# The projection behind the attention as seven products of quarters: its first two products beside the last head, the sample last

## The chip, the cores and the metric

The kernel runs on one core of one Trainium2 chip. The metric is the device time of one execution in microseconds (us). The profile is one execution taken by the hardware profiler; matrix products run on TensorE (PE), elementwise work on VectorE (DVE), ScalarE (ACT) and GpSimd (POOL), and most transfers are issued from SyncE (SP).

## The reference, cut to what matters

One encoder layer is applied to a prompt of 1024 tokens and to a sample of 256 tokens (D_MODEL = 1024, four attention heads of 256, all float32). The part that the change touches is the last line of the cross-attention, `o @ w_o`, and the residual sum behind it:

```python
def memory_cross_attention(h, mem, w_q, w_kv, w_o):
    ...
    o = jnp.einsum('bhlm,bmhd->blhd', p, v).reshape(bsz, seq, D_MODEL)
    return o @ w_o

    x = x + merged @ w_out
    x = x + memory_cross_attention(rmsnorm(x, norm_xa_w), rmsnorm(mem, norm_mem_w), xa_w_q, xa_w_kv, xa_w_o)
    h = rmsnorm(x, norm_ffn_w)
    gu = h @ ffn_w_gate_up
    x = x + (jax.nn.silu(gu[..., :D_FF]) * gu[..., D_FF:]) @ ffn_w_down
```

## The kernel before

Activations lie transposed: 128 features on the partitions, eight such tiles (`KT`), and the tokens along the free dimension in three blocks, `BLOCKS`: two of 512 (the prompt) and one of 256 (the sample). To keep float32 accuracy, each operand is split into a high part (a rounding copy on ScalarE) and a low part (a subtraction on VectorE or GpSimd, `split`), and `mm3` makes each product of three matmuls: high x high, high x low, low x high.

TensorE's order is the order of the program text, written by hand. A stage is a generator run by `K.main`; side generators (`K.side`) are advanced from it when a clock, which counts the matmuls issued so far, reaches their due time. So the attention of a head (`attend`) is threaded between the matmuls of the stage that runs as main. The other engines' instructions are ordered by the framework's planner by readiness, with the program order as priority, and each engine then runs its list in that order.

The stages around the change: `out_proj` (from line 1426) is the projection of the merged branches. For the prompt it already works by seven products of quarters (class `Seven`, line 1200, a Strassen-like scheme): the 1024x1024 weight is taken as four quarters of 512x512, the input as four quarters (two halves of the features by two token blocks), and seven products of sums of quarters (`p1` to `p7`) take the place of eight. The sums of weights (`wsum`) are on GpSimd, those of inputs (`xsum`) on VectorE; `wsplit` and `xsplit` make the high and low parts. Behind it come the four heads: each has two tiles of the query projection (`tile_of`), beside which the head before is attended. The output of heads 0 to 2 goes through the DRAM tensor `od`.

The projection behind the attention is the class `OutProj` (line 1347): eight tiles of output features by three token blocks, each a sum over eight tiles of input features. Its `begin` runs four of these (m, b) pairs over the first six input tiles beside the last head; the outputs of heads 0 to 2 are read back from `od` as `oraw` and split into `o_h`, and the last head's output is split into `o_h` directly. `run` finishes these four, does the rest, adds the residual from the DRAM tensor `x1d` on VectorE, sums the squares for the norm (`nms`), and stores `x2d`. The norm of each block (`rest`) makes the high and low parts `h3` for the FFN, which starts with `ff_first` (line 1954). `first_weights` and `after` load and split the FFN's first weights during the projection.

Of the kernel before, what the change touches and what calls it, by code (L numbers as in the profile page):

```python
# [17 lines left out]
P = 128  # L18
# [145 lines left out]
def trunk_kernel(ctx: ExitStack, tc: tile.TileContext, a):  # L164
# [40 lines left out]
    order += [(a["w_o"][m], "wp" if m < 2 else "wx") for m in range(KT)]  # L205
# [994 lines left out]
    class Seven:  # L1200


        def __init__(self, w, p, mt, smp):
            self.w, self.p, self.mt, self.smp = w, p, mt, smp
            self.raw = {}
            self.forms = [hp.tile([P, 2, 4, 512], F32R, tag=tag, name="xf") for tag in ("hi1", "lo1")]
            self.wf = {}

# [3 lines left out]
        def load(self, i, j, x, raw=None):  # L1212
            raw = self.room(f"r{i}{j}{x}") if raw is None else raw
# [3 lines left out]
        def wsplit(self, ph, src, x, eng, tags=None):  # L1217
            if x == 0:
                self.wf[ph] = []
            if ph in ("p1", "p6", "p7", "p3"):  # L1220
                hl = tuple(wp.tile([P, 1024], F32R, tag=tag, name=tag) for tag in ("whi", "wlo"))
            else:
                hl = tuple(self.room(tag, F32R) for tag in tags or (f"ah{x}", f"al{x}"))
            with ExitStack() as st:
                if ph == "p5":
                    st.enter_context(tc.issue_after(self.after))
                S.activation(hl[0], self.raw[*src, x], AF.Copy)
            eng.tensor_tensor(out=hl[1], in0=self.raw[*src, x], in1=f32(hl[0]), op=ALU.subtract)  # L1228
# [15 lines left out]
        def prep(self, ph, x):  # L1244
            w, sub = (0, 0), ALU.subtract
            if ph == "p1":
                self.wsplit(ph, (0, 0), x, V)
            elif ph == "x1":
                self.xsplit(0, 0, 0, x)
            elif ph == "x5":  # L1250
                self.xsum((0, 0), (0, 1), (0, 0), x)
                self.xsplit(1, 0, 0, x)
            elif ph == "p5":
                self.wsum((0, 1), (0, 1), (1, 1), x, ALU.add)
                self.wsplit(ph, (0, 1), x, G)
            elif ph == "c6":
                self.wsum((0, 1), (0, 1), (0, 0), x, sub)
                self.xsum((0, 0), (1, 1), (0, 0), x)
            elif ph == "p6":
                self.wsplit(ph, (0, 1), x, V)  # L1260
                self.xsplit(0, 0, 0, x)
            elif ph == "c7":
                self.wsum((0, 0), (1, 1), (0, 1), x, sub)
                self.xsum((0, 1), (1, 1), (0, 1), x)
# [357 lines left out]
    qes.close()  # L1622

# [715 lines left out]
```

## Time and profile before

| what | value |
|---|---|
| median of 3 runs | 2236.93 us (2235.42 to 2237.05) |
| the profiled execution | 2239.41 us, of which the span is 2237.6 us |
| TensorE busy in the span | 2186.0 us (98%), 12416 matmuls, mean granted clock 0.996 |
| VectorE, ScalarE, GpSimd busy | 1439.1, 829.3, 559.9 us |
| the projection behind the attention | its first matmul at 1257.04 us, the FFN's first at 1391.91 us |

Times inside the profile count from the span's start. A row of an engine's timeline gives the start, the duration, the engine and line, the operation with its output and inputs, the shapes and the count; what stands in brackets is the idle time before it and what ended that. In the busy table each row is a stretch of time with the busy time and the number of instructions of each engine, then TensorE's granted clock, and the share and rate of the DMA engines.

### The profile page before, as it was taken

To read this page: it belongs to the slowest core of one execution; us is meant where nothing else is said; L and a number is where in the kernel's file an instruction comes from. 1 tells how busy PE (TensorE), PEld (TensorE's weight loads), DVE (VectorE), ACT (ScalarE), POOL (GpSimd) and SP (SyncE) were. 2 spreads that over 40 slices of the span, in tenths; PEclk is the share of its full clock that TensorE was granted. 3 is DMA by queue.
4 is the path that set the end of the run, shared out by engine and by line. 5 is a ranking of instruction groups with operands and counts; after the bars stand their busy time and mean duration, and the time that the engine had idled before them with its cause. 6 is when DMAs were issued, how large, how long until landed. Compare 5 with 4: busy or idle time off the path is not lost.

```text
span 2237.6 us, 32329 instructions
## 1 busy us (share of the span) xinstructions
PE 2186.0 (98%) x12416; PEld 1909.1 (85%) x12416; DVE 1439.1 (64%) x2796; ACT 829.3 (37%) x1481; POOL 559.9 (25%) x358
## 2 busy tenths in 40 slices
PE   6999999999999999999999999999999999999998
PEld 5988888888888899788888888888888888888888
DVE  7767788897985874588844536743444344478575
ACT  5434143333423443124544433432223223243453
POOL 3010000000000000025331332466666666200031
PEclk9999999999999999999999999999999999999999
DMA  5222322214234454981431342222222222393531
GB/s 180 82 80 74 104 72 83 73 62 112 68 103 128 149 150 129 314 283 47 152 103 48 137 162 78 67 104 85 83 86 80 76 83 90 134 355 127 202 109 57
DMA packets 192821, 263.52 MB, mean 118 GB/s; under 512 B 72394, under 2 KB 102682, under 8 KB 192666
## 3 DMA queue, kind: packets, MB, share of 16 engines
q1 hardware_dynamic: 172826, 232.34, 31.7%
q10 hardware_dynamic: 19840, 29.11, 3.6%
q8 instruction: 97, 1.59, 0.3%
q14 instruction: 58, 0.48, 0.1%
HBM read 183.24 MB, written 78.16 MB: 117 GB/s over the span
## 4 chain that ended last, share of the span: by engine, by line
PE 77%; DVE 10%; issue 5%; DMA 4%; ACT 2%; POOL 1%; SPq 0%; ACTq 0%; POOLq 0%; DVEq 0%
PE bank L108 76%; DMA tbd<-stage 1%; PE bank L121 1%; DVE acc L615 1%; DVE xf L126 1%; DVE W L761 1%; DVE wlo L126 1%; DMA braw<-gq 1%; DVE x L1437 1%; DVE wlo L1228 1%; DMA t<-sgd 0%; DVE sw L919 0%; DVE W L764 0%; DVE U L861 0%; DVE lo L126 0%
## 5 line engine op out<-in xcount | busy, mean ns | idle before, releaser
L108 PE MATMUL bank<-hi,whi 128*128 128x512 f32 (+1 forms) x1976 | 701.8, 355 | 0.0
L108 PE MATMUL bank<-hi,wlo 128*128 128x512 f32 (+1 forms) x1976 | 687.0, 348 | 0.0
L108 PE MATMUL bank<-lo,whi 128*128 128x512 f32 (+1 forms) x1976 | 686.8, 348 | 0.0
L108 PEld LDWEIGHTS bank<-hi,wlo 128*128 128x128 f32 x1976 | 373.5, 189 | 48.8
L108 PEld LDWEIGHTS bank<-hi,whi 128*128 128x128 f32 x1976 | 374.4, 189 | 43.9 <-issue 0.2
L108 PEld LDWEIGHTS bank<-lo,whi 128*128 128x128 f32 x1976 | 374.5, 190 | 43.3 <-issue 0.2
L125 ACT ACTIVATE whi<-raw 128x1024 fp32r<-128x1024 f32 (+1 forms) x136 | 137.1, 1010 | 262.8 <-PE bank L108 221.4
L126 POOL TENSOR_TENSOR wlo<-raw,whi 128x1024 fp32r<-128x1024 f32 x65 | 157.5, 2426 | 302.8 <-ACT whi L125 302.8
L108 PE MATMUL bank<-bhl,whi 128*128 128x512 f32 x408 | 125.9, 390 | 0.0
L126 DVE TENSOR_TENSOR wlo<-raw,whi 128x1024 fp32r<-128x1024 f32 (+1 forms) x71 | 81.6, 1151 | 43.7 <-ACT whi L125 36.7
L126 POOL TENSOR_TENSOR wlo<-x,whi 128x1024 fp32r<-128x1024 f32 x40 | 97.5, 2436 | 46.8 <-ACT whi L125 46.7
L2009 DVE TENSOR_TENSOR x<-x,bank 128x512 f32<-128x512 f32 x21 | 14.4, 688 | 125.3 <-ACT x L1804 125.3
L108 PEld LDWEIGHTS bank<-bhl,whi 128*128 128x128 f32 x408 | 76.4, 188 | 16.3 <-ACT whi L125 0.3
L615 DVE SCALAR_TENSOR_TENSOR acc<-craw,sm,acc 128x510 f32<-128x510 f32 (+1 forms) x96 | 73.5, 766 | 20.5 <-ACT acc L613 19.1
L1817 DVE SCALAR_TENSOR_TENSOR t<-t,x 128x512 f32<-128x512 f32 x42 | 64.4, 1534 | 28.4 <-ACT t L1816 28.4
L108 PE MATMUL bank<-bhl,wlo 128*128 128x512 f32 x204 | 79.6, 390 | 0.5 <-DVE wlo L126 0.5
L761 DVE TENSOR_TENSOR W<-W,UT 128x2 f32<-128x2 f32 (+30 forms) x155 | 73.0, 471 | 11.0 <-DMA W<-in_eye 6.7
L250 DVE TENSOR_TENSOR nacc<-nacc,nsq 128x512 f32<-128x512 f32 (+1 forms) x68 | 57.9, 852 | 34.5 <-ACT nsq L249 33.4
L125 ACT ACTIVATE whi<-x 128x1024 fp32r<-128x1024 f32 (+1 forms) x48 | 49.0, 1025 | 79.9 <-PE bank L108 73.7
L1826 DVE SCALAR_TENSOR_TENSOR t<-bank,t 128x512 f32<-128x512 f32 (+1 forms) x44 | 24.5, 558 | 82.6 <-PE bank L108 82.6
L978 ACT ACTIVATE gs<-bank 128x512 f32<-128x512 f32 (+1 forms) x60 | 31.2, 520 | 124.9 <-PE bank L108 119.6
L881 POOL COPY UT<-U 64x512 f32<-64x512 f32 x20 | 13.9, 699 | 247.2 <-PE bank L108 245.6
(372 smaller groups left out, 4606.6 us busy)
## 6 DMA issues: line engine op xcount, KB each, us to landing
raw<-in_w_gu SPq DMA_DIRECT2D x44, 512.0 KB, 3.4
braw<-gq SPq DMA_DIRECT2D x14, 1024.0 KB, 6.5
raw<-in_w_g SPq DMA_DIRECT2D x20, 512.0 KB, 3.3
gq<-t SPq DMA_DIRECT2D x33, 256.0 KB, 2.0
gtd<-gs ACTq DMA_DIRECT2D x32, 256.0 KB, 2.0
w<-in_w_dn SPq DMA_DIRECT2D x8, 1024.0 KB, 12.3
raw<-in_w_qkv SPq DMA_DIRECT2D x12, 512.0 KB, 3.5
gq<-r SPq DMA_DIRECT2D x22, 256.0 KB, 2.1
```

The lines of the kernel that those rows point to most:

```text
L108: self.nc.tensor.matmul(out, l, r, start=start, stop=stop, skip_group_check=more)
L121: self.nc.tensor.transpose(out, x, ident)
L125: self.last_hi = self.nc.scalar.activation(hi, src, AF.Copy).ins
L126: (eng or self.nc.vector).tensor_tensor(out=lo, in0=src, in1=f32(hi), op=ALU.subtract)
L250: (eng or V).tensor_tensor(out=self.acc, in0=self.acc, in1=sq, op=ALU.add)
L615: V.scalar_tensor_tensor(out=dst, in0=src, scalar=wj, in1=dst, op0=ALU.mult, op1=ALU.add)
L761: V.tensor_tensor(out=t3, in0=u3[:, i:, c:].rearrange("p j c -> p c j"), in1=XL[:, 32 * i + i : 32 * i + 32].unsqueeze(1).to_broadcast([P, ...
L978: S.activation(t, ps, AF.Tanh, scale=0.5)
L1228: eng.tensor_tensor(out=hl[1], in0=self.raw[*src, x], in1=f32(hl[0]), op=ALU.subtract)
L1437: V.scalar_tensor_tensor(out=d, in0=ps, scalar=0.5, in1=d, op0=ALU.mult, op1=ALU.add)
L1817: V.scalar_tensor_tensor(out=t, in0=t, scalar=1.0, in1=src, op0=ALU.add, op1=ALU.mult)
L1826: V.scalar_tensor_tensor(out=out, in0=u, scalar=sign, in1=t, op0=ALU.mult, op1=ALU.mult)
```

## The change

`OutProj`, `FIRST_PS`, `first_weights` and `after` go. The prompt's part of `o @ w_o` is made by `Seven` too, through the functions `o_begin` and `o_proj`; `Seven` gets its rooms and engines as arguments (`raws`, `places`, `engs`), and the steps of its `prep` are named by kind (`w` split of a weight, `x` split of an input, `s` sum of weights, `d` difference of inputs) and product. The heads' outputs for the prompt are kept unsplit in `mo`: those of heads 0 to 2 are read from `od`, the last head's are copied there by ScalarE. `o_begin` runs the products p1 and p5 beside the last head and copies their sums to `s12` (ScalarE); `o_proj` runs p6, p2, p7, p4 and p3, adds the kept sums into the residual (four operations on VectorE, four on GpSimd), and then runs the four sample products from `od`. The heads' keys and values move to the pool `comb`, whose rooms later hold quarters of `w_o`, their forms and FFN operands. The FFN's first weights are loaded and split among the sample's products. The norms get waiting times of their own, `LAGO`.

```diff
-    order += [(a["w_o"][m], "wp" if m < 2 else "wx") for m in range(KT)]
...
-                for mt in range(2):
-                    vs = slice((2 * g + mt) * 256 + j * P, (2 * g + mt) * 256 + (j + 1) * P)
...
-                if o_h is None:
+                if mt is None or b == 2:
                     oo = tp.tile([P, 512], F32, tag="oo", name="oo", bufs=2)[:, :n]
                     S.activation(oo, po, AF.Copy)
                     S.dma_start(od[2 * h + j, :, t0 : t0 + n], oo)
                 else:
-                    hi, lo = o_h[b]
-                    split(hi[:, 2 * h + j, :], lo[:, 2 * h + j, :], po)
+                    S.activation(mt[b][:, 2 * h + j, :], po, AF.Copy)
                 yield A4
+            if b == 1 and then is not None:
+                then()
...
+            mo = [hp.tile([P, KT, 512], F32, tag=tag, name="mo") for tag in ("hi0", "lo0")]
+            wq = [tq.tile([P, 2, NTOK], F32R, tag=f"q{i}", name="wq") for i in range(2)]
+            tag = lambda *x: tuple(f"t{i}" for i in x)
+            form = (tag(4, 6), tag(5, 7))
+            oo_ = Seven(
+                a["w_o"], tpool, mo, None, {(0, 1): tag(0, 1), (1, 1): tag(2, 3), (1, 0): tag(8, 9)},
+                dict(p5=lambda x: tuple(t[:, x, :1024] for t in wq), p2=form, p4=form, s01=(tag(0, 2), tag(1, 3)),
+                     s10=lambda x: (slot(8 + x), slot(10 + x)), s00=form),
+                dict(p5=G, p2=G, p4=G, s01=G, s10=G))
+            for k in range(0, 6, 2):
+                for b in range(2):
+                    SY.dma_start(mo[b][:, k : k + 2, :], od[k : k + 2, :, 512 * b : 512 * b + 512].rearrange("k p t -> p k t"))
+                if k == 0:
+                    for x in range(2):
+                        oo_.load(0, 0, x, K.raw()[:, :1024])
+                elif k == 2:
+                    for x in range(2):
+                        oo_.load(0, 1, x)
+                        oo_.load(1, 1, x)
+            oo_.preps("wp1", "xp1")
+            def then():
+                oo_.preps("dp6", "xp6")
...
+    def kept(i, scale=1.0):
+        return lambda m, ps: S.activation(s12[i][:, m, :], ps, AF.Copy)
+    def o_begin():
+        oo_.preps("dp5", "xp5")
+        for y in range(2):
+            oo_.prep("sp5", y)
+            oo_.prep("wp5", y)
+        oo_.preps("sp6")
+        yield from oo_.prompt("p1", 0, pa, True, kept(0))
+        oo_.preps("wp6")
+        yield from oo_.prompt("p5", 1, pa, False, kept(1))
...
-    K.main(op.begin())
+    K.main(o_begin())
     K.finish(at_side)
...
+    def second_weights():
+        for n, (i, j) in enumerate(((8, 9), (10, 11))):
+            gu_w[1, 3 * n] = slot(i), slot(j)
+            split(*gu_w[1, 3 * n], gu_raw[1][n], G)
+        g, u = gu_raw[1]
+        for x, y in ((u[:, 512:], u[:, :512]), (u[:, :512], g[:, :512]), (g[:, :512], u[:, 512:]), (g[:, 512:], g[:, :512])):
+            G.tensor_tensor(out=x, in0=x, in1=y, op=ALU.add)
+    def o_proj():
+        x = [p.tile([P, KT, n], F32, tag=f"x{b}", name=f"x{b}") for b, (p, (_, n)) in enumerate(zip((x0p, xhp, x2p), BLOCKS))]
+        for b in (1, 0, 2):
+            t0, n = BLOCKS[b]
+            SY.dma_start(x[b], x1d[:, :, t0 : t0 + n])
...
+        for y in range(2):
+            oo_.load(1, 0, y)
+        pa = [bank(pm) for _ in range(4)]
+        both("wp2", "xp2")
+        both("sp7", "dp7")
+        add(1, 0, 1, V)
+        add(0, 0, 0, V)
+        yield from oo_.prompt("p6", 0, pa, True, into(0, 1, False))
+        both("wp7", "xp7")
+        both("dp4", "sp3")
+        add(1, 1, 1, G)
+        add(0, 1, 0, G)
+        smp = [hp.tile([P, KT, NS], F32R, tag=tag, name="smp") for tag in ("lo2", "hi2")]
...
+        pb = [bank() for _ in range(4)]
+        yield from oo_.prompt("p2", 1, pb, True, into(0, 0, True))
+        both("wp4", "xp4")
+        for y in range(2):
+            oo_.load(0, 1, y, K.raw()[:, :1024])
+        yield from oo_.prompt("p7", 0, pa, False, into(1, 1, True))
+        both("wp3", "xp3")
+        oo_.preps("ws01")
+        for k in (4, 0):
+            sl = slice(k, k + 4)
+            split(smp[0][:, sl, :], smp[1][:, sl, :], f32(smp[1][:, sl, :]), G)
+        yield from oo_.prompt("p4", 1, pa, False, into(1, 0, True))
...
+        norm_of(0)
+        oo_.preps("ws10")
+        pb = [bank(pm) for _ in range(4)]
+        yield from oo_.prompt("p3", 0, pb, True, into(0, 1, True))
+        norm_of(1)
+        yield from oo_.sample("p4", 1, into_s(1, False))
+        oo_.preps("ws00")
+        gu_load(0, wp)
+        yield from oo_.sample("s01", 0, into_s(1, True))
+        for i in (0, 3):
+            gu_w[0, i] = pair_of(wp)
+            split(*gu_w[0, i], gu_raw[0][i // 3], G)
+        gu_load(1, wp)
+        comb_rooms(b12, ((0, 1), (2, 3)))
+        yield from oo_.sample("s10", 1, into_s(0, False))
+        second_weights()
+        yield from oo_.sample("s00", 0, into_s(0, True))
...
-    K.main(op.run(x1d, 1.0, S_FFN, x2p, x2d, sinks, first_weights, after))
-    room, x1 = op.x[0], op.x[1]
+    K.main(o_proj())
+    room, x1 = ox[0], ox[1]
...
+LAGO = (5000, 7000, 6000)
```

298 lines of the change are left out of this document (129 added, 169 removed).

## The prediction

> **What bounds the kernel now.** I read the page first, then the busy table by stage, then the rows of each engine around the stage that the change rebuilds.
>
> ```profile
> PE 2186.0 (98%) x12416; PEld 1909.1 (85%) x12416; DVE 1439.1 (64%) x2796; ACT 829.3 (37%) x1481; POOL 559.9 (25%) x358
> ...
> PEclk9999999999999999999999999999999999999999
> ...
> PE 77%; DVE 10%; issue 5%; DMA 4%; ACT 2%; POOL 1%; SPq 0%; ACTq 0%; POOLq 0%; DVEq 0%
> ```
>
> TensorE is the bound: it is busy nearly all of the span, at full clock, and 77% of the chain that ended last is its own. So a matmul taken out is worth its slot, as long as nothing else becomes late. Whether something does is a question for the stage. The busy table, in order: the earlier stage that already multiplies by seven products; 26 us inside it; the last head until the projection is alone; the rest of the projection; the first part of the FFN.
>
> ```profile
> core 0: us, PE busy (x) PEld busy (x) DVE busy (x) ACT busy (x) POOL busy (x), PEclk, DMA share, GB/s
> 993.40:1094.80 101.40, 100.70 (x531) 85.91 (x530) 81.08 (x86) 48.79 (x64) 49.14 (x19) 1.00 0.32 112
> 1003.20:1029.20 26.00, 26.00 (x138) 22.34 (x137) 24.91 (x16) 9.40 (x9) 24.68 (x8) 1.00 0.26 95
> 1257.04:1291.80 34.76, 31.92 (x187) 27.09 (x186) 23.90 (x53) 14.99 (x37) 9.96 (x5) 1.00 0.33 110
> 1291.80:1392.10 100.30, 100.22 (x542) 87.05 (x542) 51.24 (x85) 29.86 (x46) 36.04 (x18) 1.00 0.30 106
> 1392.10:1436.00 43.90, 42.56 (x225) 36.44 (x225) 42.80 (x66) 22.13 (x36) 13.92 (x8) 1.00 0.23 77
> ```
>
> Today's projection (fourth row) loses nothing on TensorE, and VectorE has half its time free there. TensorE waits only beside the last head. From its rows come the slots and those waits:
>
> ```profile
> 1225.89 0.40 PE L108 MATMUL bank<-hi,whi 128*128 128x512 f32 x1
> ...
> 1229.75 0.39 PE L108 MATMUL bank<-hi,wlo 128*128 128x512 f32 x1
> ...
> 1235.52 0.28 PE L108 MATMUL bank<-hi,whi 128*128 128x256 f32 x1
> ...
> 1237.55 0.28 PE L108 MATMUL bank<-hi,wlo 128*128 128x256 f32 x1
> ...
> 1265.34 1.99 PE L108 MATMUL bank<-kv,q 128*128 128x256 f32 x12 [1.79 <-DVE e L1528]
> 1290.02 0.39 PE L108 MATMUL bank<-pt,kv 128*128 128x256 f32 x1 [0.53 <-ACT pt L125]
> 1290.81 0.39 PE L108 MATMUL bank<-pt,kv 128*128 128x256 f32 x1 [0.40 <-DVE pt L126]
> ```
>
> Eighteen matmuls of 512 columns begin 3.86 us apart from first to last: 0.227 us each. For 256 columns it is 2.03/17 = 0.119 us. The waits are 1.79 + 0.53 + 0.40 = 2.7 us.
>
> **What the change takes from TensorE.** The prompt's part is 8 x 8 x 2 x 3 = 384 matmuls of 512 today and 7 x 4 x 4 x 3 = 336 after: 48 x 0.227 = **-10.9 us**. The sample stays at 192 of 256. Today 54 + 18 matmuls (14.4 us) of the projection lie beside the last head; so its attention takes 34.8 - 14.4 - 2.7 = 17.6 us. After, the first two products (96 x 0.227 = 21.8 us) lie there, and the join comes at 39.4 us from 1257.04 plus waits. Four more prompt products of 10.9 us follow (43.6), then p3, the sample, and the norms' small matmuls.
>
> **What it puts on VectorE and GpSimd.** This is where I see the danger. In the 26 us of the second row above, the two engines ran these:
>
> ```profile
> 1000.80 2.40 POOL L1228 TENSOR_TENSOR al<-r,ah 128x1024 fp32r<-128x1024 f32 x1
> 1003.16 5.77 POOL L1239 TENSOR_TENSOR r<-r,raw 128x1024 f32<-128x1024 f32 x2
> 1008.89 6.73 POOL L1239 TENSOR_TENSOR raw<-r,r 128x1024 f32<-128x1024 f32 x2
> 1016.79 2.40 POOL L1228 TENSOR_TENSOR al<-r,ah 128x1024 fp32r<-128x1024 f32 x1 [1.17 <-ACT ah L1227]
> 1019.27 3.27 POOL L1239 TENSOR_TENSOR r<-r,r 128x1024 f32<-128x1024 f32 x1
> 1022.50 3.37 POOL L1228 TENSOR_TENSOR al<-r,ah 128x1024 fp32r<-128x1024 f32 x1
> 1025.95 3.27 POOL L1239 TENSOR_TENSOR r<-r,r 128x1024 f32<-128x1024 f32 x1
> ...
> 1004.25 2.41 DVE L126 TENSOR_TENSOR xf<-mt,xf 128x1024 fp32r<-128x1024 f32 x1 [5.66 <-ACT xf L125]
> 1006.69 3.32 DVE L1242 TENSOR_TENSOR mt<-mt 128x1024 f32<-128x1024 f32 x1
> 1009.94 3.42 DVE L126 TENSOR_TENSOR xf<-mt,xf 128x1024 fp32r<-128x1024 f32 x1
> ...
> 1013.88 2.47 DVE L1437 SCALAR_TENSOR_TENSOR x<-bank,x 128x512 f32<-128x512 f32 x4
> ...
> 1016.88 6.75 DVE L1228 TENSOR_TENSOR wlo<-r,whi 128x1024 fp32r<-128x1024 f32 x2
> 1023.55 3.41 DVE L1242 TENSOR_TENSOR mt<-mt 128x1024 f32<-128x1024 f32 x1
> ...
> 1036.87 1.21 DVE L126 TENSOR_TENSOR xf<-mt,xf 128x1024 fp32r<-128x1024 f32 x1
> 1038.00 0.68 DVE L1437 SCALAR_TENSOR_TENSOR x<-bank,x 128x512 f32<-128x512 f32 x1
> ```
>
> A VectorE operation on two SBUF operands of 128x1024 takes 1.13 us when GpSimd rests (1036.87 to 1038.00) and up to 3.42 us beside it. A GpSimd one takes 2.40 us, or up to 3.37. From 1003.16 to 1029.22 there are eight of GpSimd's and six of VectorE's: 8 x 2.40 + 6 x 1.13 = 26.0 us in 26.06 us. They do not overlap at all; their times add. Evacuations with an operand in PSUM do overlap (x<-bank, four in 2.47 us while GpSimd works). So the two engines have one common budget for such operations, and I count the new stage against it.
>
> The Trainium skill, "SBUF — State Buffer", section "Who interferes with whom", says that VectorE and GpSimd share a port pair that whoever starts first holds for the whole instruction, while ScalarE and TensorE never wait. If they merely shared bandwidth, the port term below would be near zero and the sum would be that of the first rival; the 26.0 us speak for the lock.
>
> Until the join (39.4 us): GpSimd the weight sums and splits sp5, wp5, sp6, six of 2.40 = 14.4 us; VectorE wp1's second half, xp1, dp5, xp5, wp6, dp6, xp6, thirteen of 1.13 = 14.7 us. Together 29.1: fits.
>
> From the join to the start of p3 (43.6 us): GpSimd wp2, sp7, sp3, the four adds of the kept products and wp4, twelve = 28.8 us; VectorE xp2, dp7, its four adds, wp7, xp7, dp4, xp4, wp3, xp3, twenty = 22.6 us, and ten norm sums of 512 at about 0.6 (half of 1.13) = 6.0 us. Together 57.4 us in 43.6: **+13.8 us**. Each of the next products waits for some of these operations, so the excess lands on TensorE. Two corrections of opposite sign: sp7, dp7 and dp4 (9.4 us) could run ahead of the join, as raw<-r,r did at 1008.89; then +4.4 is left. And ws01 and the sample's splits (9.6 us), needed only later, stand before p4 in the order and could be served first: +23.4. I keep 13.8, about midway, because dp4 and half of dp7 need the last head's output and cannot run far ahead, and keep both ends for the range.
>
> Behind p3: ws01, sample splits, ws10 and the first FFN weights are eight of 2.40 on GpSimd, the rest of the norms and splits (512 columns at about 0.6) about 19 us, 38 us in all against 34 us of matmuls plus some 4 of norm matmuls: even, no term.
>
> **The last head.** Today VectorE's lo-parts of oraw sit ahead of the first scores (the 1.79 us). After, xp1, wp1, dp5 and xp5, eight operations, beside six of GpSimd's, sit there. Bounds: -2.7 if all waits go; +8 if the six of GpSimd (14.4 us) all come first and four PSUM banks cover some 6 us. I take **+2**: near today's row, a little more queued.
>
> **The FFN's start.** second_weights (two splits and four half sums, 2 x 2.41 + 5.59 = 10.4 us of GpSimd) runs at 1377.90 to 1388.9 today and would run beside the FFN's first part, where VectorE is busy 42.80 of 43.90 us:
>
> ```profile
> 1377.90 2.41 POOL L126 TENSOR_TENSOR wlo<-raw,whi 128x1024 fp32r<-128x1024 f32 x1 [22.43 <-ACT whi L125]
> 1380.78 2.41 POOL L126 TENSOR_TENSOR wlo<-raw,whi 128x1024 fp32r<-128x1024 f32 x1 [0.47 <-ACT whi L125]
> 1383.27 5.59 POOL L1749 TENSOR_TENSOR raw<-raw 128x512 f32<-128x512 f32 x4
> ```
>
> Bounds 0 to 10.4; **+3**, since the products that use these forms come some 30 us after the FFN's start.
>
> **Loads at nothing.** The quarters `mo` are loaded on SP once head 3's first block has been projected, 10 us before 1257.04; behind them in SP's queue stand the weight loads for p5, due 20 us later. The x loads must wait for rooms that p5's weights hold:
>
> ```profile
> 1246.97 0.60 ACT L1587 ACTIVATE q<-bank 128x512 fp32r<-128x512 f32 x1 [0.76 <-PE bank L108]
> ...
> DMA to landing us min/median/max: 3.7/6.0/9.5
> ```
>
> The landing line is that of today's x loads. Landed some 6 to 13 us behind the join, they are there before p7 needs p6's banks (21.8 us). Were that cover gone, VectorE's queue would stand still with xp7 and wp7 behind the blocked add: up to +5. The norms' and attention's output copies on ScalarE (14.99 of 34.76 us busy) cost nothing.
>
> **Sum.** -10.9 + 13.8 + 2 + 3 = +7.9 us on the profiled execution of 2239.41 us (span 2237.6): 2247.3. The median of the runs is 2236.93, 2.5 us lower; so **2244.8 us**.
>
> **Rivals.** *Faster: the budget never binds.* The order of VectorE and GpSimd is made by readiness; if it hoists all of the 9.4 us and puts off the 9.6, 4.4 us or less is left, and the head's waits shrink: -10.9 + 4.4 - 2 = -8.5, and -13.6 if nothing waits at all. It decides where the waits of the whole stage stay under 6.4 us (10.9 less 4.5). For it: the 26 us of full budget in the earlier stage cost TensorE next to nothing (100.70 busy of 101.40). Against it: that stage has sample products between the prompt ones, giving it time, and 19 GpSimd operations; here there are some 26 of that size or more, packed closer. *A draw:* the excess eats about what the matmuls give, within 4.5 us. *Much slower: the queues block.* GpSimd serves the operations needed last first (+23.4 in place of 13.8), and VectorE stands at an add that waits for x: -10.9 + 23.4 + 2 + 3 = +17.5, to +28 with 5 for the loads and 5 more for the clock. It decides once GpSimd's ws01 comes ahead of VectorE's wp3.
>
> On that clock, the trace has one piece:
>
> ```profile
> 2230.00:2237.60 7.60, 1.19 (x4) 0.90 (x4) 2.05 (x5) 0.38 (x1) 2.09 (x3) 0.50 0.42 138
> ```
>
> Behind idle stretches TensorE's granted clock is 0.50 there; in the stage itself no wait is over 1.79 us and the clock is 1.00. A few waits of 4 to 5 us could thus cost more than their length; I estimate up to 5 us and put it into the upper end only.
>
> The Trainium skill, "TensorE: Matmul & The Clock Gate", Part 1, says that about 3.4 us of idleness halves the clock until about 3.4 us of work have passed; by that, three waits of 4.6 us would cost an estimated 3 x 1.7 = 5.1 us more, and the sum would be +13.
>
> **How the numbers follow.** A difference under 0.2%, 4.5 us, is about what a measurement of this kernel cannot tell from none. Forecast case (+4.5 to +15, its own range 2241.4 to 2252): 0.45. Faster: 0.30. Draw: 0.12. Much slower: 0.13. So slower 0.58, same 0.12, faster 0.30. The likeliest gives 2244.8. The range goes from -9 (2228) to +22 (2259), which leaves out the far ends of the first and the last rival, under 2 in 10.
>
> **What would show it.** In the changed profile: 48 matmuls fewer; between the join and p3, GpSimd and VectorE both busy almost throughout, VectorE operations of 2.4 to 3.5 us, and TensorE waits at the first matmuls of p7, p4 and p3 released by xf, wlo or x, some 14 us in all. If TensorE is without waits there, the port term is wrong and the change is faster. If VectorE's waits end on x<-x1d, the loads were it. If the waits stand among the scores, the head was it.

## The result, and the profile after

The changed kernel takes 2271.05 us (median of four runs, 2266.53 to 2273.83) against 2236.99 us of the kernel before: a ratio of 1.0152, 95% interval 1.0132 to 1.0171. It is 34 us slower, where 7.9 us were forecast, and lies above the range. The profiled execution took 2273.01 us, with a span of 2271.2 us.

From the page of the changed kernel: busy times, the row of granted clocks, and the shares of the chain that ended last.

```profile
PE 2187.3 (96%) x12368; PEld 1907.9 (84%) x12368; DVE 1505.2 (66%) x2827; ACT 852.7 (38%) x1508; POOL 595.8 (26%) x368
...
PEclk9999999999999999999999899999999999999999
...
PE 76%; DVE 12%; issue 5%; DMA 3%; ACT 2%; POOL 1%; SPq 0%; ACTq 0%; POOLq 0%; DVEq 0%
```

The 48 matmuls are gone (12416 to 12368), but TensorE is busy as long as before: those that are left took longer. One of the forty slices shows a clock under 0.9. The busy table by stage follows: the last head up to the join, the join to p3, p3 and the sample, the start of the FFN; between them four pieces around waits, and last the whole stretch.

```profile
1255.98:1316.62 60.64, 42.72 (x214) 35.98 (x213) 47.23 (x65) 28.68 (x52) 24.23 (x8) 0.83 0.07 25
1261.00:1279.00 18.00, 1.74 (x9) 1.15 (x8) 17.94 (x13) 4.88 (x9) 18.00 (x7) 0.68 0.00 0
1279.00:1290.00 11.00, 9.34 (x38) 7.89 (x38) 8.31 (x20) 4.99 (x12) 1.58 (x1) 0.59 0.01 2
1316.62:1373.27 56.65, 46.11 (x194) 37.35 (x193) 53.66 (x37) 21.39 (x28) 45.30 (x14) 0.91 0.46 153
1338.50:1348.41 9.91, 0.07 (x2) 0.03 (x1) 9.91 (x5) 1.06 (x1) 9.83 (x4) 0.71 0.17 53
1348.41:1373.27 24.86, 24.16 (x96) 19.48 (x97) 24.00 (x25) 13.36 (x18) 13.77 (x5) 0.91 0.28 85
1373.27:1415.94 42.67, 39.51 (x272) 36.81 (x273) 33.71 (x64) 19.86 (x30) 17.90 (x9) 0.96 0.50 173
1415.94:1450.00 34.06, 26.93 (x111) 21.52 (x110) 34.04 (x55) 14.13 (x26) 11.86 (x10) 0.90 0.11 39
...
1250.00:1460.00 210.00, 171.25 (x898) 146.68 (x898) 180.43 (x228) 91.84 (x145) 102.78 (x42) 0.90 0.30 105
```

TensorE rests 210.00 - 171.25 = 38.75 us in the last row. Its timeline says where (of the rows with a wait only the two of 1.66 and 0.70 us are left out):

```profile
1278.80 1.65 PE L108 MATMUL bank<-t,q 128*128 128x256 f32 x6 [16.26 <-DVE e L1467]
...
1348.41 1.19 PE L108 MATMUL bank<-xf,whi 128*128 128x512 f32 x2 [9.84 <-DVE x L1703]
...
1387.30 1.01 PE L108 MATMUL bank<-cst,nst 128*128 128x128 f32 x3 [3.16 <-DVE nst L228]
...
1426.65 0.58 PE L108 MATMUL bank<-cst,nacc 128*128 128x1 f32 x4 [3.04 <-DVE nacc L249]
...
1440.56 0.68 PE L108 MATMUL bank<-cst,nst 128*128 128x128 f32 x4 [4.09 <-DVE nst L228]
```

One wait stands among the scores, one at p7, three at the norms. In the same stretch before, it rested 4.26 us:

```profile
1250.00:1460.00 210.00, 205.74 (x1126) 177.84 (x1125) 130.19 (x217) 78.65 (x133) 82.92 (x42) 1.00 0.30 103
```

So the waits cost +34.5 us. The lowered clock costs another part: the working time of a stretch times (1 - clock), summed over the rows above, is 1.74 x 0.32 + 9.34 x 0.41 + 24.16 x 0.09 + 39.51 x 0.04 + 26.93 x 0.10 = 10.8 us. With these, 33.6 us of span leave 33.6 - 34.5 - 10.8 = -11.7 for the work itself, where -10.9 was forecast. This ledger (waits, clock, rest) is used on every run below; the clock's part is summed over pieces of 2 us.

Why the scores were late: GpSimd and VectorE during the long wait.

```profile
1256.35 6.49 POOL L1243 TENSOR_TENSOR t<-t,t 128x1024 f32<-128x1024 f32 x2 [40.68 <-DMA t<-in_w_o]
1262.80 6.61 POOL L1232 TENSOR_TENSOR wq<-t,wq 128x1024 fp32r<-128x1024 f32 x2
1269.37 6.60 POOL L1243 TENSOR_TENSOR t<-t,raw 128x1024 f32<-128x1024 f32 x2
1275.93 4.65 POOL L1243 TENSOR_TENSOR raw<-t,t 128x1024 f32<-128x1024 f32 x2
...
1316.80 6.54 POOL L1232 TENSOR_TENSOR t<-t,t 128x1024 fp32r<-128x1024 f32 x2 [36.22 <-ACT xf L125]
...
1257.16 3.43 DVE L1246 TENSOR_TENSOR mo<-mo 128x1024 f32<-128x1024 f32 x1
...
1260.85 3.07 DVE L1232 TENSOR_TENSOR wlo<-raw,whi 128x1024 fp32r<-128x1024 f32 x1
1263.85 3.37 DVE L1246 TENSOR_TENSOR mo<-mo 128x1024 f32<-128x1024 f32 x1
1267.13 3.36 DVE L126 TENSOR_TENSOR xf<-mo,xf 128x1024 fp32r<-128x1024 f32 x1
1270.42 0.41 DVE L1462 TENSOR_REDUCE st<-bank 128x1 f32<-128x256 f32 x1
1270.75 3.02 DVE L126 TENSOR_TENSOR xf<-mo,xf 128x1024 fp32r<-128x1024 f32 x1
1273.70 2.29 DVE L1463 TENSOR_TENSOR st<-st,rstd 128x1 f32<-128x1 f32 x1
```

GpSimd works without a pause through the wait, and each of VectorE's operations on two SBUF operands lasts about as long as one of GpSimd's: they take turns (the lock, below). VectorE runs its list in order, and wp1, dp5 and xp5 stand ahead of the scores' sums. Even 128x1 (row 1273.70) takes 2.29 us.

GpSimd's rows also show when this work fell there. It stood idle for 40.68 us until a load of `w_o` landed, at the moment when the scores came; and four of its eight operations, 1269.37 to 1280.58, are the sums for p6 and p7, which start at the join (1316.62), after 36.22 us in which GpSimd is idle again. No run moved the load or these four.

### The profile page after: what moved, and what is told of

Its sections match the earlier page's. It is cut to its first block, busy times and chain, and to the rows that moved or that the text cites. A ratio compares the mean times of both kernels' runs of the same rounds, so it can differ in the third digit from the quotient of the medians.

```text
span 2271.2 us, 32346 instructions
## 1 busy us (share of the span) xinstructions
PE 2187.3 (96%) x12368; PEld 1907.9 (84%) x12368; DVE 1505.2 (66%) x2827; ACT 852.7 (38%) x1508; POOL 595.8 (26%) x368
## 4 chain that ended last, share of the span: by engine, by line
PE 76%; DVE 12%; issue 5%; DMA 3%; ACT 2%; POOL 1%; SPq 0%; ACTq 0%; POOLq 0%; DVEq 0%
PE bank L108 75%; DVE xf L126 1%; PE bank L121 1%; DVE nacc L249 1%; DVE wlo L1232 1%; DVE acc L614 1%; DMA braw<-gq 1%; DVE wlo L126 1%; DVE x L1345 1%; DMA stage<-gtd 1%; DVE lo L126 0%; DVE x L1724 0%; DVE sw L918 0%; DVE U L860 0%; DVE x L1703 0%
## 5 line engine op out<-in xcount | busy, mean ns | idle before, releaser
L108 PE MATMUL bank<-hi,whi 128*128 128x512 f32 (+1 forms) x1280 | 474.8, 371 | 0.0
L108 PE MATMUL bank<-hi,wlo 128*128 128x512 f32 (+1 forms) x1280 | 460.4, 360 | 0.0
L108 PE MATMUL bank<-lo,whi 128*128 128x512 f32 (+1 forms) x1280 | 460.2, 360 | 0.0
L108 PEld LDWEIGHTS bank<-hi,wlo 128*128 128x128 f32 x1280 | 242.7, 190 | 37.2
L108 PEld LDWEIGHTS bank<-hi,whi 128*128 128x128 f32 x1280 | 243.5, 190 | 31.1 <-ACT whi L125 0.2
L108 PEld LDWEIGHTS bank<-lo,whi 128*128 128x128 f32 x1280 | 243.5, 190 | 31.0 <-issue 0.2
L108 PE MATMUL bank<-hi,t 128*128 128x512 f32 (+1 forms) x1008 | 231.1, 318 | 0.0
L108 PEld LDWEIGHTS bank<-hi,t 128*128 128x128 f32 x1008 | 170.6, 190 | 15.2
L108 PE MATMUL bank<-lo,t 128*128 128x512 f32 (+1 forms) x504 | 160.7, 319 | 0.0
L108 PE MATMUL bank<-t,whi 128*128 128x512 f32 x352 | 109.4, 392 | 0.0
L2046 DVE TENSOR_TENSOR x<-x,bank 128x512 f32<-128x512 f32 x21 | 14.4, 688 | 127.6 <-ACT x L1841 127.6
L108 PE MATMUL bank<-xf,whi 128*128 128x512 f32 x256 | 83.3, 408 | 11.0 <-DVE x L1703 10.5
L108 PEld LDWEIGHTS bank<-bhl,whi 128*128 128x128 f32 x408 | 76.4, 188 | 16.5 <-ACT whi L125 0.5
```

The lines of the kernel that those rows point to most:

```text
L108: self.nc.tensor.matmul(out, l, r, start=start, stop=stop, skip_group_check=more)
L2046: V.tensor_tensor(out=c22, in0=c22, in1=pe, op=ALU.add)
```

## The experiments

Each was timed against the kernel before on the same chip, whose own median lay between 2236.2 and 2238.6 us; differences of 2 or 3 us between comparisons say little. Waits and clock are those of the ledger, for 1250 to 1460 us of the profiled execution, whose time lies up to 6.5 us off the run's median (e5).

| run | median us | ratio to before, 95% interval | waits | clock | span less both |
|---|---|---|---|---|---|
| before | 2236.99 | 1 | 4.3 | 0.0 | 2233.3 |
| changed | 2271.05 | 1.0152 (1.0132 to 1.0171) | 38.8 | 10.8 | 2221.6 |
| e1_head_no_gpsimd | 2253.84 | 1.0075 (1.0059 to 1.0091) | 24.8 | 10.0 | 2218.1 |
| e2_prep_behind_scores | 2259.34 | 1.0100 (1.0080 to 1.0120) | 25.9 | 11.2 | 2222.4 |
| e12_scalar_form | 2265.63 | 1.0140 (1.0115 to 1.0164) | 36.2 | 10.5 | 2217.1 |
| e9_keep_busy | 2273.59 | 1.0162 (1.0143 to 1.0180) | 25.3 | 13.7 | 2237.2 |
| e14_keep_busy_2 | 2270.70 | 1.0150 (1.0134 to 1.0167) | 21.3 | 7.2 | 2238.9 |
| e4_no_adds | 2260.14 | 1.0106 (1.0083 to 1.0128) | 29.9 | 10.2 | 2224.1 |
| e3_adds_vector | 2269.44 | 1.0147 (1.0129 to 1.0166) | 39.6 | 7.8 | 2220.1 |
| e6_adds_deferred | 2263.21 | 1.0116 (1.0098 to 1.0135) | 31.5 | 13.7 | 2221.1 |
| e5_norm_lags | 2271.58 | 1.0145 (1.0127 to 1.0164) | 39.3 | 11.3 | 2225.7 |
| e10_no_second_weights | 2264.07 | 1.0123 (1.0108 to 1.0138) | 36.3 | 6.4 | 2218.2 |
| e7_all_repairs | 2252.80 | 1.0066 (1.0050 to 1.0083) | 21.7 | 7.2 | 2219.9 |
| e8_all_and_sample | 2253.73 | 1.0071 (1.0054 to 1.0088) | 21.8 | 8.9 | 2220.3 |
| e11_best_try | 2252.47 | 1.0072 (1.0055 to 1.0089) | 21.0 | 6.3 | 2219.9 |
| e13_order_everywhere | 2252.13 | 1.0067 (1.0053 to 1.0080) | 20.0 | 8.6 | 2220.6 |
| e15_order_no_sample | 2253.17 | 1.0069 (1.0057 to 1.0081) | 20.6 | 11.7 | 2219.0 |

The last column is the test of the ledger: 2217 to 2226 us in every run of the change, and higher only in the two runs with unused matmuls in them (60 and 87 of 0.227 us, 13.6 and 19.7 us; 2223.6 and 2219.2 without). The change did save 8 to 16 us of TensorE's work. Within that spread of 9 us, what differs is waits and clock. The ledger says where the time of a run goes; what a change to it gives back only a run can show.

### Beside the last head: the lock or the order?

e1_head_no_gpsimd leaves GpSimd out of this stage: the sums of weights for p5, p6 and p7 are not made, and p5's low part is a copy.

```diff
             elif kind == "s":
-                self.wsum(...)
+                if ph == "p3" or self.after is not None: self.wsum(...)   # none for p5, p6, p7
...
-            G.tensor_tensor(out=hl[1], in0=raw, in1=f32(hl[0]), op=ALU.subtract)   # wp5
+            S.activation(hl[1], raw, AF.Copy)
```

> Beside the last head GpSimd has nothing to do for the projection: the weight sums of p5, p6 and p7 are left out (those products then multiply unsummed quarters), and p5's low weight part is a ScalarE copy instead of a subtraction. VectorE's list of operations is the same as in the changed kernel. Theory 1, the common budget: VectorE's eight preparations fall from 2.3-3.4 us to about 1.1 us each, so the scores' sums start some 13 us earlier: the wait for e in front of the scores (17.9 us) falls to 4 us or less, the stretch of lowered clock behind it (0.59 to 0.68 today) goes, and the run is some 18 to 22 us shorter than the changed kernel: about 2249 to 2253 us. Theory 2, the order alone (VectorE's preparations stand in front of the scores whatever they last, or wait for loads or for ScalarE): the wait stays at 8 us or more, and the gain is under 10 us. The waits at p7 stay near 10 us in both.

e2_prep_behind_scores keeps all the work and moves four operations of VectorE's list.

```diff
-        oo_.preps("dp5", "xp5")
...
+        for n, _ in enumerate(oo_.prompt("p1", 0, pa, True, kept(0))):
+            if n == 6:
+                with tc.issue_after(K.e_ins):   # the last e of the first scores
+                    oo_.preps("dp5", "xp5")
+            yield
```

> All work is kept; only the place of two preparations changes: the differences dp5 and the splits xp5 (four operations of VectorE on two SBUF operands) are issued behind the first head block's scores on VectorE instead of in front of them. GpSimd's list is the same. Theory 1, the common budget with VectorE's list run in order: four operations of about 3.3 us leave the way of the first scores, so the wait for e falls from 17.9 us to 3 to 6 us; the operations are paid later, beside p1, where they may cost up to 5 us before p5. In sum 8 to 16 us shorter than the changed kernel: 2255 to 2263 us. Theory 2 (what is late is something in front of these, such as the loads of mo or the splits of p1): the wait stays over 12 us and the time within 4 us.

e12_scalar_form edits the 128x1 product alone.

```diff
-            V.tensor_tensor(out=st[:, 0:1], in0=st[:, 3:4], in1=r, op=ALU.mult)
+            V.tensor_scalar(out=st[:, 0:1], in0=st[:, 3:4], scalar1=r, scalar2=None, op0=ALU.mult)
```

> The changed kernel with one edit: the scores' product of two 128x1 operands on VectorE (rows of 2.29 us and of 1.56 us for two, beside GpSimd, in front of the first scores) is written as a product with a per-partition scalar. Theory 1, the lock concerns operations with two tensors in SBUF: these fall to about 0.16 us each, the wait for e falls from 17.9 to about 14 us, and the run is 3 to 5 us shorter than the changed kernel: 2266 to 2268 us. Rival, VectorE's next operation on two tensors takes over the wait for GpSimd: the wait for e stays over 16 us and the time within 2 us.

The first waits among the scores, in e1, e2 and e12 in this order, from TensorE's timeline:

```profile
1261.10 1.05 PE L108 MATMUL bank<-t,q 128*128 128x256 f32 x6 [2.61 <-DVE e L1472]
```

```profile
1266.47 2.01 PE L108 MATMUL bank<-t,q 128*128 128x256 f32 x7 [3.60 <-DVE e L1467]
```

```profile
1273.81 1.65 PE L108 MATMUL bank<-t,q 128*128 128x256 f32 x6 [14.46 <-DVE e L1467]
...
1271.10 6.64 POOL L1243 TENSOR_TENSOR raw<-t,t 128x1024 f32<-128x1024 f32 x2
1272.14 0.20 DVE L1463 TENSOR_SCALAR st<-st,rstd 128x1 f32<-128x1 f32 x1
```

With GpSimd silent, the same list of VectorE in the same order lets the scores through after 2.6 us in place of 16.3: the lock is the cause. With GpSimd at work but four operations out of the way, it is 3.6 us: the order decides whether TensorE feels the lock. The long wait needs both. e2 gains 11.7 us by two moved steps; e1 gains 17.2, slightly under its forecast, since its clock came back less than thought (10.0 us are still lost). The 128x1 operation lasts 0.20 us in its scalar form although GpSimd is in the middle of its own, and the waits for e fall from 17.9 to 15.0 us (14.46 + 0.50). The run's own gain is not clear of the noise: 5.4 us by the medians, 2.7 by the ratios, whose intervals overlap. The lock concerns operations on two tensors. The Trainium skill, "SBUF — State Buffer", section "Who interferes with whom", says the same: a VectorE instruction with at most one SBUF input, outside the two-port modes, does not contend with GpSimd, and one with two SBUF inputs does where GpSimd's instruction reads SBUF.

### What a rest costs beyond its length

e9_keep_busy and e14_keep_busy_2 put unused matmuls into the wait among the scores.

```diff
+            if h == HEADS - 1 and (b, c) == (1, 0):   # e14: 75 here, and 12 at (1, 1)
+                for _ in range(60):
+                    K.nc.tensor.matmul(pa[3], ..., start=True, stop=True)
             ps = bank()[:, :NMEM]
```

> The changed kernel with sixty matmuls of 512 columns more, in front of the score matmul at which TensorE waits 16.3 us beside the last head; they go into a bank whose content is not used. They are the only difference. Theory 1, the wait itself is set by VectorE and the lowered clock behind it is a second loss: the sixty take about 60 x 0.227 = 13.6 us of the wait, so 2 to 3 us of it are left, the clock of 0.59 in the 11 us behind it goes up to nearly 1.00, and the run is about 4 us shorter than the changed kernel in spite of 60 matmuls more: span 2266 to 2268 us. Rival, the lowered clock costs nothing beyond the wait (VectorE goes on setting the pace of the scores): the span stays within 1 us of 2271.

> The changed kernel with 75 and 12 unused matmuls of 512 columns in front of the two score matmuls at which TensorE waits beside the last head, so that it never rests there. Theory 1, the lowered clock comes from the rests, also from one of 2 to 3 us (the first such run left rests of 2.95 and 2.34 us, and its clock fell to 0.51): now the slots of p1's matmuls behind the scores stay at 0.23 us instead of 0.43, and from the first matmul of p1 to the wait at p7 the time is 2 to 3 us shorter than the 92.4 us of the changed kernel. Rival, the clock falls for another reason (a budget that earlier work has used up): the slots go to 0.43 all the same.

TensorE's timeline behind these scores, first in the changed kernel, then in e9 (with a row of its busy table), then in e14; the duration of two matmuls shows the clock.

```profile
1255.98 0.68 PE L108 MATMUL bank<-xf,whi 128*128 128x512 f32 x2
...
1284.85 1.05 PE L108 MATMUL bank<-xf,whi 128*128 128x512 f32 x2
```

```profile
1281.78 0.98 PE L108 MATMUL bank<-t,q 128*128 128x256 f32 x6 [2.95 <-DVE e L1469]
...
1285.09 1.65 PE L108 MATMUL bank<-t,q 128*128 128x256 f32 x6 [2.34 <-DVE e L1469]
```

```profile
1285.10:1290.00 4.90, 4.90 (x15) 4.14 (x16) 4.33 (x14) 1.86 (x6) 0.00 (x0) 0.51 0.00 0
```

```profile
1254.35 0.68 PE L108 MATMUL bank<-xf,whi 128*128 128x512 f32 x2
...
1282.64 0.63 PE L108 MATMUL bank<-xf,whi 128*128 128x512 f32 x2
...
1345.32 1.19 PE L108 MATMUL bank<-xf,whi 128*128 128x512 f32 x2 [9.84 <-DVE x L1710]
```

e9 did not bring what theory 1 said (the median of its spans is 2271.8 us, the rival's figure), but it is no test of either: I had left 2.95 and 2.34 us of rest, and the clock fell to 0.51 all the same, at 1283.1, some 0.35 us into the second rest. In e14, where the only rest left there is one of 0.48 us, the slots stay at their 0.23 us, so the rests lower the clock and nothing else that the stretch does. From p1's first matmul to the first behind the wait at p7 it takes 1345.32 - 1254.35 = 90.97 us against 1348.41 - 1255.98 = 92.43 in the changed kernel: 1.5 us less, where 2 to 3 were expected, with 87 matmuls more. The ledger's clock falls from 10.8 to 7.2 us, but the run as a whole is not measurably shorter (2270.70 against 2271.05 us), and the wait at p7 is 9.84 us as in the changed kernel. So a clock regained is not all time gained.

A shorter rest can be enough. In e13 (below) TensorE rested 1.97 us ahead of 1342.14, and from 1343.6 to 1346.8 its clock was 0.50; from e13's busy table:

```profile
1344.00:1346.00 2.00, 2.00 (x6) 1.60 (x5) 1.83 (x2) 2.00 (x3) 1.37 (x1) 0.50 0.61 182
```

The rest of 1.79 us beside the last head in the kernel before was followed by a clock of 1.00. No run shows what decides between the two. The Trainium skill, "TensorE: Matmul & The Clock Gate", Part 1, puts the fall behind some 3.4 us of idleness; here one rest of 1.97 us was enough in e13, and two of 2.95 and 2.34 us with 0.98 us of scores between them in e9, where the 4.9 us of work behind them ran at 0.51. The measurement decides.

### Between the join and p3: the adds

e4_no_adds drops the eight adds; e3_adds_vector moves GpSimd's four to VectorE; e6_adds_deferred has all eight on VectorE, each pair ahead of the product that ends its quarter.

```diff
-        add(1, 0, 1, V)            # e4: none of the four lines
-        add(0, 0, 0, V)
...
-        add(1, 1, 1, G)            # e3: G becomes V in these two
-        add(0, 1, 0, G)
...
+        add(0, 0, 0, V)            # e6: ahead of p2
+        add(1, 1, 1, V)            # e6: ahead of p7
+        add(1, 0, 1, V)            # e6: ahead of p4
+        add(0, 1, 0, V)            # e6: behind wp3, xp3
```

> The eight adds of kept sums are left out altogether (the prompt's result lacks p1's and p5's share); the loads of x, all products and all preparations stay. Theory 1, the common budget: 4 x 2.4 + 4 x 1.1 = 14.1 us of budget go, the wait at p7 (10.5 us) falls to 1 us or less, and the run is 11 to 15 us shorter than the changed kernel: 2256 to 2260 us. Rival, the loads of x arrive late: the evacuations of p6 still add into x and wait for it, and the wait at p7 stays over 5 us. The wait of 17.9 us among the scores stays in both.

> The four of the eight adds of kept sums that GpSimd does (13.29 us of it beside p6 and p2) go to VectorE. Theory 1, the common budget: each costs the pair of engines 1.1 us instead of 2.4 us or more, so the pair needs some 5 us less before p7, and the 10.5 us wait at p7 falls to about 5 us; 5 to 8 us shorter than the changed kernel: 2263 to 2266 us. Rival, VectorE alone is the bound there: it gets four more operations of 1.1 to 3.4 us, and the wait grows to 12 us or more: 2271 to 2277 us.

> All work is kept; the eight adds of kept sums are all on VectorE and each pair stands just ahead of the product that needs it last (before p2, p7, p4 and p3) instead of all of them ahead of p2; the sample's load and split stand behind them. Theory 1, order inside a budget that is full but not overfull (the run with the adds on VectorE in their old place only slid the wait from p7 to p4): neither wait is left over 4 us, and the run is 6 to 12 us shorter than the changed kernel: 2259 to 2265 us. Rival, the budget is overfull whatever the order: the wait slides to p4 or p3, its sum stays near 10 us, and the time is within 3 us of the run with the adds moved to VectorE alone (2269).

The longest wait between the join and p3, in e4 (with VectorE's first use of x), e3 and e6:

```profile
1353.31 3.92 PE L108 MATMUL bank<-xf,t 128*128 128x512 f32 x16 [2.46 <-DVE x L1703]
...
1333.98 0.69 DVE L1703 TENSOR_TENSOR x<-x,bank 128x512 f32<-128x512 f32 x1 [0.16 <-DMA x<-x1d]
```

```profile
1358.96 3.33 PE L108 MATMUL bank<-xf,t 128*128 128x512 f32 x7 [9.69 <-DVE x L1703]
```

```profile
1354.22 3.32 PE L108 MATMUL bank<-xf,t 128*128 128x512 f32 x7 [3.70 <-DVE x L1703]
```

Without the adds, the wait of 9.84 us at p7 is gone and 2.46 us are left at p4; 10.9 us are gained, just short of the forecast. VectorE waited 0.16 us for the loads of x: these were not it. With the adds on VectorE in their old place the wait only slid from p7 to p4 (9.69 us), because the evacuations that p4 needs stand behind them, and behind norm sums and splits, in VectorE's list. Neither of my two forecasts had that. Put later, the same adds leave a wait of 3.70 us there, and 7.8 us are gained. So this stage's budget is tight, and the order decides what is late.

### The norms and the FFN's start

e5_norm_lags raises three waiting times of the norms. e10_no_second_weights leaves out GpSimd's work on the FFN's second group of weights: the splits become copies, and the half sums are not made.

```diff
-LAGO, LAGS2 = (5000, 7000, 6000), (2800, 9500, 7000)
+LAGO, LAGS2 = (5000, 7000, 11000), (8000, 9500, 13000)      # e5
...
-            split(*gu_w[1, 3 * n], gu_raw[1][n], G)          # e10: two ScalarE copies
-            G.tensor_tensor(out=x, in0=x, in1=y, op=ALU.add) # e10: none of the four
```

> All work is kept; only three of the waiting times of the norms are raised (first block's second wait 2800 to 8000, the sample's first 6000 to 11000 and second 7000 to 13000), so that TensorE comes to the norms' small matmuls later and works at something else meanwhile. Theory 1: the waits of 3.2, 3.0 and 4.1 us in front of these matmuls are only badly timed visits; they go, and with them the lowered clock of 0.86 in the 25 us around the last two (3.5 us): 9 to 13 us shorter than the changed kernel, 2258 to 2262 us. Rival, the norms are really late and the FFN needs them: the same waits come back in front of the FFN's products, and the time stays within 3 us of the changed kernel.

> The GpSimd work for the FFN's second group of weights is left out (two splits become ScalarE copies, four half sums are dropped: 16 us of GpSimd at 1406 to 1425 us; the FFN's values for that group are then wrong in part). Theory 1, this work is what makes the sample's sums of squares and the norm late at the start of the FFN: VectorE's operations there fall from 1.5 to 2.4 us to 0.4 to 0.7 us, the waits of 3.0 and 4.1 us fall by 4 us or more together, and the run is 4 to 8 us shorter than the changed kernel: 2263 to 2267 us. Rival, the norm's chain is late because its ten short steps stand between VectorE's long operations for the FFN: the wait of 4.1 us stays over 3 us and at most 3 us are gained.

In e5, from TensorE's timeline:

```profile
1405.43 4.82 PE L108 MATMUL bank<-smp,t 128*128 128x256 f32 x21 [4.09 <-DVE bank L226]
...
1448.64 1.19 PE L108 MATMUL bank<-cst,nst 128*128 128x128 f32 x4 [5.67 <-DVE nst L228]
```

The rival held: a later visit only changes the name of the wait. The first norm keeps its PSUM bank until its root is done, and now a sample product waits for a bank; the sample's norm is needed by the FFN and is late. In e10 the wait of 3.04 us for the sums of squares is gone and the clock loses 4.4 us less: 7.0 us are gained, as theory 1 said. But 3.75 us are left at the sample's second norm matmul, as its rival said:

```profile
1430.63 1.20 PE L108 MATMUL bank<-cst,nst 128*128 128x128 f32 x4 [3.75 <-DVE nst L228]
```

Both causes are there. GpSimd's second weights delay the sums, and the short steps of the root (L226 to L228) stand between VectorE's operations of 1.2 us for the FFN, here in the changed kernel:

```profile
1435.40 0.16 DVE L227 TENSOR_TENSOR bank<-bank,nst 128x2 f32<-128x2 f32 x1
1435.47 1.22 DVE L126 TENSOR_TENSOR lo<-x,hi 128x1024 fp32r<-128x1024 f32 x1
1436.60 0.15 DVE L228 SCALAR_TENSOR_TENSOR nst<-bank,nst 128x2 f32<-128x2 f32 x1
```

### All together

e7_all_repairs joins e2, e12, e6 and e5. e8_all_and_sample adds the sample's product with quarter (1, 0) behind p2; e11_best_try loads and splits its input earlier and has other waiting times. e13_order_everywhere is e11 with three more changes of order and another waiting time, and e15_order_no_sample is e13 without the sample's move.

```diff
+        yield from oo_.sample("p2", 1, into_s(0, False), sh)   # e8, e11, e13: behind p2's prompt product
...
+            eng = G if ph == "p1" and x == 1 else V            # e13, e15
...
+                with tc.issue_after(K.pt_ins):                 # e13, e15: behind the first split of probabilities
+                    oo_.preps("dp5", "xp5")
...
+        with tc.issue_after(K.y_ins):                          # e13, e15: behind the sample's root
+            make_r1()
```

> Four repairs at once, all work kept: dp5 and xp5 behind the first scores, the adds deferred on VectorE, the raised waiting times of the norms, and the scores' product of two 128x1 operands (2.29 us behind a GpSimd operation) written as a product with a per-partition scalar. If the causes are separate, the gains add: 12 (measured) + 11 + 9 + 2 = 34 us, about 2237 us, level with the kernel before (2233 to 2243). If one cause is behind all (for instance the clock alone), the sum falls short: 2245 us or more. For the 128x1 operation alone: in the trace it should last about 0.15 us beside GpSimd if the lock concerns operations on two tensors only, 0.7 us or more if any operation on SBUF is locked out.

> The four repairs, and the sample's product with quarter (1, 0) runs directly behind p2 with p2's forms, its input in two free rooms, so that one load and one split of that quarter go (2 x 2.4 us of GpSimd) and p7's preparations get 5.8 us more. The work on TensorE is the same. Theory 1: whatever is left of the waits at p7 and p4 goes, and the run is 2 to 6 us shorter than with the four repairs alone: 2231 to 2238 us, level with or faster than the kernel before. Rival: the cover between p3 and the FFN shrinks from 23 us to 17 us and the second block's norm becomes late: waits of 3 to 6 us in front of the FFN, no gain over the four repairs.

> The four repairs with the sample's product behind p2, its input loaded and split earlier (ahead of p6 in the order), and waiting times for the norms between the old and the raised ones, so that the chain of the sample's norm stands ahead of the FFN's sums on VectorE. Theory 1: the 3.8 us of waits at that product and some 3 to 5 us in front of the FFN go: 2244 to 2249 us, still 7 to 12 us over the kernel before, since the 5 us of waits beside the last head and VectorE's full list between the join and p3 stay. Rival, every repair only moves the place where VectorE is late: 2251 us or more.

> The best try with three more edits of order, all work kept: beside the last head GpSimd makes the second low part of p1's weights, and dp5 and xp5 stand behind the first split of probabilities on VectorE instead of behind the first scores; at the start of the FFN the sums for r1 stand behind the ten short steps of the sample's norm; its second waiting time is 13000. Theory 1, what is left of the waits is VectorE's order and not its load: the waits of 2.9 and 3.0 us beside the head and 10.9 us in front of the FFN fall to 6 us together, the clock loses about 4 us, and by the ledger 2221 + 10 + 4 = 2235 us of span: level with the kernel before, 2232 to 2240 us. Rival, VectorE is loaded to the full and any repair moves its lateness on: 2247 us or more.

> The same edits of order as in e13, but the sample's four products all stay behind p3 as in the changed kernel. It tells what the place of the sample's product is worth once the rest is in order. Theory 1: 3 to 6 us between p6 and p3 come back as waits at p4 and at the first norm (3.7 and 2.6 us in the run with the four repairs): 2237 to 2245 us. Rival: the place of the sample's product is worth nothing: within 2 us of e13.

All five end between 2252.1 and 2253.7 us. e7's forecast of 2237 us fell short, and the time is in its rival's range (2245 or more). That does not show one cause behind all; the gains overlap: its four repairs, one by one, gave 11.7 + 7.8 - 0.5 + 5.4 = 24.4 us by the medians (nothing from the norms' waiting times), and together 18. The rivals of e8, e11, e13 and e15 held: the place of the sample's product is worth nothing, and VectorE's lateness moves on. What is left in e13: the stretch, and four of its waits.

```profile
1250.00:1460.00 210.00, 189.98 (x988) 160.05 (x987) 169.28 (x242) 96.64 (x151) 99.22 (x44) 0.94 0.30 105
```

```profile
1279.95 1.22 PE L108 MATMUL bank<-xf,wq 128*128 128x512 f32 x2 [3.45 <-DVE xf L126]
...
1342.14 13.20 PE L108 MATMUL bank<-xf,t 128*128 128x512 f32 x48 [1.97 <-DVE x L1716]
...
1422.76 0.58 PE L108 MATMUL bank<-hi,whi 128*128 128x256 f32 x1 [3.19 <-ACT hi L125]
...
1429.39 0.58 PE L108 MATMUL bank<-lo,whi 128*128 128x256 f32 x1 [2.55 <-POOL lo L126]
```

The rests are many and small now; some 8 of the 20.0 us lie at the FFN's first sample product. VectorE is busy 169.28 of 210 us (130.19 before). Whether less work on VectorE and GpSimd at the FFN's start would close the gap was not tried on e13; e10 speaks for it. No version beat the kernel before, and what would is open.

## Why the prediction was wrong, step by step

Held against the profile's places, the working and the measurement part in this way:

| stretch | by the prediction | measured | difference |
|---|---|---|---|
| up to p1's first matmul | 1257.04 | 1255.98 | -1.1 |
| to the join | 39.4 + 2.7 + 2 = 44.1 | 60.64 | +16.5 |
| join to p3 | 43.6 + 13.8 = 57.4 | 56.65 | -0.7 |
| p3 to the FFN | 34 + 4 = 38 | 42.67 | +4.7 |
| FFN's start to the end | 845.7 + 3 | 2271.2 - 1415.94 = 855.3 | +6.6 |

The 845.7 us are 2237.6 less 1391.91, the FFN's first matmul before. The differences are 26.0 us, and 7.9 + 26.0 is the measured +33.6 within rounding.

**The last head** is the step that failed: taken at +2, with +8 as its upper bound, it cost some 18 (16.5 + 2), of it 4.4 by the clock. The mechanism named there was right (operations of both engines queue ahead of the first scores), and so was the rule that their times add. But the +2 followed today's row and no sum, and the bound counted GpSimd's 14.4 us alone, less 6 us of cover. With VectorE's own 8 x 1.13 = 9.0 us by the same rule it is 14.4 + 9.0 - 6 = 17.4 us; the waits for e are 17.9. That this is so near is in part luck, since the list was another: three of VectorE's eight had run before GpSimd began, and GpSimd did a seventh. By the rows it is 7 x 2.40 + 5 x 1.13 = 22.5 us (21.9 pass from 1256.35 to the first e at 1278.28), less the 6.2 us in which TensorE still had work: 16.3, and the first wait is 16.26. The stage's total was checked against its 39 us ("fits"), and not the place in it where somebody waits. e1 and e2 show the two parts of this, and e12 the lock on a single operation.

**Join to p3**, the danger that was named, came near the 13.8: 13.05 us over the 43.6, 10.5 of it waits at p7 and p3 and 2.2 clock. The waits stand less spread than expected: nearly all at p7. That the size fits is in part luck. The 13.8 was the middle between +4.4 and +23.4, and the order that the upper end stood for did come (ws01's halves start at 1346.66 and 1357.93 on GpSimd, wp3's at 1359.45 and 1370.18 on VectorE) without its price. And e6, with all the work kept and some 5 us less by these prices since all eight adds are VectorE's, has 3.70 us as its longest wait there. e4 shows that the adds are the price, and e3 and e6 that their place is part of it.

**p3 to the FFN** was held even; 3.16 us at the first norm and 1.6 us of clock are the difference. **The FFN's start**, taken at +3 for second_weights: the norms' waits there are 7.1 us against 1.33 before, and 2.7 us go to the clock. e10 puts 7.0 us on second_weights, inside the bounds of 0 to 10.4; the rest, the sample's norm that comes last, had no term.

**The clock** was left out of the sum, with up to 5 us at the upper end. By the ledger it costs 10.8. The likeliest case needed it too, as each case with waits has it.

**Right** were the matmuls (-10.9; -11.7 by the ledger), the loads of x at nothing (0.16 us in e4), that the kernel gets slower, and the sign that the head was it if the waits stand among the scores. The faster rival's condition, waits under 6.4 us, is far off even in e13 (20.0). The slowest rival (+17.5 to +28) was nearest in size, but not by its mechanism: the queue that blocked was VectorE's among the scores. Its clause that several waits of 4 to 5 us cost more than their length was right.

## What to carry to other kernels

A budget that two engines share is to be checked at every place where a third engine waits for something in it, with the operations of both engines that stand ahead there, and not over a whole stage. An operation that is not needed yet is put behind those that are waited for (e2: 11.7 us for two moved steps), and a product with a column is written with a per-partition scalar (2.29 to 0.20 us). Rests of TensorE are priced above their length: here the ledger has 10.8 us of clock on 38.8 us of rest, though filling the rests among the scores (e14) gave only 1.5 us of it back.

## What the hardware showed beside that

Two rests of 2.95 and 2.34 us, after more than 14 us of unbroken work, lowered the granted clock to 0.51 for 4.9 us of work (e9), and one of 1.97 us lowered it to 0.50 for 3.2 us (e13). A VectorE operation of 128x1 on two SBUF operands took 2.29 us beside GpSimd (the changed kernel), and 0.20 us with a per-partition scalar (e12).
